# A causal depthwise convolution of width 31: from two chunks on VectorE and six on TensorE to all eight on TensorE, in blocks of 16 channels and 8 shifts

## The chip, the core and the metric

The program runs on one core of a Trainium2 chip. TensorE (PE; its weight loads are shown apart, as PEld) multiplies matrices, VectorE (DVE), ScalarE (ACT) and GpSimd (POOL) work elementwise, and SyncE (SP) issues most of the DMAs. Each engine takes its own instructions in order. The metric is the device time of one execution in microseconds, the median of several runs.

## The reference

One inference step of a two-layer decoder over a new prompt of 512 positions and 8 x 4 sample positions, 544 columns in all, 1024 channels. Layer 0 is a conformer convolution, layer 1 an attention; each is followed by a feed-forward network (FFN). The change lies in layer 0:

```python
def causal_dwconv(x_ext, w, b):           # w: (31, 1024)
    y = lax.conv_general_dilated(x_ext, w[:, None, :], window_strides=(1,), padding='VALID', ...,
                                 feature_group_count=c)
    return y + b

def conformer_conv(h, past, w_in, b_in, w_dw, b_dw, ln_g, ln_b, w_out, b_out):
    u = h @ w_in + b_in
    a, gate = jnp.split(u, 2, axis=-1)
    glu = a * jax.nn.sigmoid(gate)
    ext = jnp.concatenate([past, glu], axis=1)
    y = causal_dwconv(ext, w_dw, b_dw)
    y = jax.nn.silu(layer_norm(y, ln_g, ln_b))
    return y @ w_out + b_out, ext[:, -(CONV_WIDTH - 1):]
```

Each output of a channel is the sum over 31 shifts of that channel's glu times a tap. For the prompt, `past` is zero; the samples have their own past of 30 rows. Layer norm runs over the 1024 channels of a position.

## The kernel before

Activations lie transposed: channels on the 128 partitions, in eight chunks `c`, positions along the free dimension, in two streams `h`: positions 0 to 255 (SA), and 256 to 511 with the 32 samples behind them (SB, 288 columns). Weights come from DRAM as 1 MB blocks `raw`; ACT makes their rounded high part `whi` (line 369), DVE the rest `wlo` (line 372), and a product is three matmuls for each of eight k (lines 700 to 702), into a PSUM tile `acc`. GpSimd's queue issues the loads of `raw` of this layer.

Layer 0 is written as a list of operations given to a planner, `Plan`. Each operation has an engine, a cost, and what it reads and writes; `Plan.run` takes for each engine the ready operation that starts soonest, weighted by rank, and so fixes the order in which every engine's instructions are written (SP's too). On the chip each engine keeps that order and waits at its head.

The steps are: `conv_in` (four products of the input projection, then `glu`, which writes the gated values into `ext_p` behind 30 columns of zeros), the depthwise convolution of the prompt, `conv_sample` (the samples, on DVE: one product of 992 columns and one sum per chunk), `add_sum` (adds the chunks' results `yc`, the same memory as `ext_p`, into `ysum` on DVE), `layer_norm(h)`, and the output projection's products into `xT`. `layer_norm(0)` starts with a matmul by a matrix of 1/1024 (line 870), which gives the mean of every position; then come eight subtractions (line 878), squares, their sums over the channels by four matmuls (line 888), root, reciprocal, eight products (line 899), SiLUs (line 901), and the high and low parts `XH` and `XL` (lines 903 and 904), which the output products take. `layer_norm(1)` does the same for the second half and the samples.

The convolution of the prompt is done in two ways. Chunks 0 and 1 go to DVE (`conv_vector`): 31 operations over 256 or 512 columns, each multiplying a shifted view of `ext_p` with one tap and adding it up (lines 781 to 788). Chunks 2 to 7 go to PE: `shifted` stores a half chunk in DRAM (`glu`) and loads it four times, each time one position further, so that a tile `rep` has four shifts of 32 channels on its 128 partitions, for four groups of channels; `diagonal` makes on ACT, for each group and each of eight steps, a matrix `wdg` of 128 x 32 with the taps on its four diagonals (192 small operations, line 823); `conv_tensor` runs 8 steps x 4 groups of matmuls over 256 columns (line 837; each shows as two records), and ACT evicts the block with the bias into `yc` (line 842). Four `rep` buffers and two PSUM banks `av` go round.

## Time and profile before

| what | us |
|---|---|
| median of three runs (lowest, highest) | 1287.97 (1287.44, 1288.45) |
| the profiled execution | 1289.36 |
| its span on the core | 1287.7 |
| PE busy in the span | 1270.2 (99%) |
| DVE, ACT, POOL busy | 980.4, 713.5, 152.4 |
| matmuls of the convolution (line 837) | 42.9 |
| taps on ACT (line 823) | 42.6 |
| convolution on DVE (line 784, two shapes) | 27.9 + 21.7 |
| first mean over the channels, first half (line 870) | at 135.11 |
| the same, second half and samples | at 165.70 |

The convolution layer takes about the first 219 us; what follows is the first FFN. A line like "L837 PE MATMUL av<-rep,wdg ... x768 | 42.9, 380" is a group: 768 records of line 837, which write `av` from `rep` and `wdg`, busy for 42.9 us together, 380 ns each, overlapping. "[1.30 <-DVE ysum]" in a timeline is idle time of that engine before the instruction, and what ended it.

### The profile page before, as it was taken

The page shows a single profiled execution, that of the slowest core. Times are in us where ns is not written, and L with a number is a line of the kernel's source. Part 1 is how long each engine was busy: PE and PEld are TensorE (multiplying, and loading weights), DVE is VectorE, ACT ScalarE, POOL GpSimd, SP SyncE. Part 2 cuts the span into 40 slices and gives each one's busy share as a digit, 9 for nine tenths or more (in the row PEclk, how much of TensorE's full clock was granted, in tenths as well). Part 3 has the DMA queues.
Part 4 walks back from the last instruction along what each step waited for, and adds up shares of the span by engine and source line. Part 5 has one row for each costly group of instructions (what it writes and reads, how often), then busy time and mean ns, then how long its engine had stood idle before and what let it go on. Part 6 is the DMA issues. An engine that isn't in the chain of part 4 may idle for free.

```text
span 1287.7 us, 26497 instructions
## 1 busy us (share of the span) xinstructions
PE 1270.2 (99%) x10860; PEld 1215.5 (94%) x10860; DVE 980.4 (76%) x1671; ACT 713.5 (55%) x1440; POOL 152.4 (12%) x289
## 2 busy tenths in 40 slices
PE   9999999999999999999999999999999999999997
PEld 8997789999999999999988888889999999999997
DVE  6899875979987877768366586756988987887864
ACT  7596574645644545445366587754645555455453
POOL 4000014101001000000142123100111011000000
PEclk9999999999999999999999999999999999999999
DMA  8465233133232223244553445333133233233221
GB/s 225 123 175 140 83 100 114 34 92 107 91 117 91 91 93 115 67 133 141 175 159 120 140 140 175 104 113 99 50 100 92 93 114 115 67 116 94 80 76 70
DMA packets 119402, 142.38 MB, mean 111 GB/s; under 512 B 5357, under 2 KB 110469, under 8 KB 119010
## 3 DMA queue, kind: packets, MB, share of 16 engines
q1 hardware_dynamic: 110350, 111.89, 28.1%
q0 software_dynamic: 8640, 28.78, 7.1%
q8 instruction: 85, 1.39, 0.5%
q14 instruction: 35, 0.29, 0.1%
q10 hardware_dynamic: 292, 0.02, 0.0%
HBM read 129.34 MB, written 12.18 MB: 110 GB/s over the span
## 4 chain that ended last, share of the span: by engine, by line
PE 85%; DVE 10%; issue 2%; ACT 1%; DMA 1%; DVEq 0%; POOL 0%; ACTq 0%; POOLq 0%
PE acc L1545 5%; PE acc L1543 5%; PE acc L1544 5%; PE acc L700 4%; PE acc L701 4%; PE acc L702 3%; PE acc L459 3%; PE acc L460 3%; PE acc L461 3%; PE tr L1544 3%; PE tr L1543 3%; PE tr L1545 3%; PE av L1341 3%; PE acc L1969 3%; PE av L1343 3%; PE av L1342 3%
## 5 line engine op out<-in xcount | busy, mean ns | idle before, releaser
L372 DVE TENSOR_TENSOR wlo<-raw,whi 128x1024 fp32r<-128x1024 f32 (+2 forms) x245 | 257.4, 1052 | 46.0 <-ACT whi L369 44.5
L369 ACT CAST whi<-raw 128x1024 fp32r<-128x1024 f32 (+2 forms) x245 | 223.5, 914 | 117.1 <-PE av L1342 24.6
L700 PE MATMUL acc<-XH,whi 128*128 128x288 f32 (+1 forms) x384 | 114.5, 298 | 0.0
L701 PE MATMUL acc<-XL,whi 128*128 128x288 f32 (+1 forms) x384 | 110.9, 289 | 0.1
L702 PE MATMUL acc<-XH,wlo 128*128 128x288 f32 (+1 forms) x384 | 110.4, 288 | 0.1
L1969 PE MATMUL acc<-XH,whi 128*128 128x256 f32 (+1 forms) x264 | 82.8, 314 | 0.6 <-ACT XH L2274 0.6
L1543 PE MATMUL acc<-TH,whi 128*128 128x272 f32 x288 | 82.9, 288 | 0.0
L1545 PE MATMUL acc<-TH,wlo 128*128 128x272 f32 x288 | 82.8, 288 | 0.0
L1544 PE MATMUL acc<-TL,whi 128*128 128x272 f32 x288 | 82.7, 287 | 0.0
L1579 ACT COPY G<-acc 128x272 f32<-128x272 f32 (+1 forms) x72 | 26.7, 371 | 94.9 <-PE acc L1545 94.9
L1341 PE MATMUL av<-HH,whi 128*128 128x288 f32 x256 | 76.2, 298 | 0.2
L1970 PE MATMUL acc<-XL,whi 128*128 128x256 f32 (+1 forms) x264 | 76.2, 289 | 0.1
L1971 PE MATMUL acc<-XH,wlo 128*128 128x256 f32 (+1 forms) x264 | 75.9, 287 | 0.0
L1342 PE MATMUL av<-HL,whi 128*128 128x288 f32 x256 | 75.5, 295 | 0.0
L1343 PE MATMUL av<-HH,wlo 128*128 128x288 f32 x256 | 75.3, 294 | 0.0
L700 PEld LDWEIGHTS acc<-XH,whi 128*128 128x128 f32 x384 | 72.2, 188 | 2.8 <-issue 1.6
L701 PEld LDWEIGHTS acc<-XL,whi 128*128 128x128 f32 x384 | 72.3, 188 | 1.0 <-DVE XL L952 0.3
L702 PEld LDWEIGHTS acc<-XH,wlo 128*128 128x128 f32 x384 | 72.2, 188 | 0.3 <-DVE wlo L372 0.3
L1341 PE MATMUL tr<-HH,whi 128*128 128x256 f32 x256 | 71.9, 281 | 0.0
L1342 PE MATMUL tr<-HL,whi 128*128 128x256 f32 x256 | 71.9, 281 | 0.0
L1343 PE MATMUL tr<-HH,wlo 128*128 128x256 f32 x256 | 71.5, 279 | 0.0
L1482 DVE SCALAR_TENSOR_TENSOR cv<-G,fprm,cv 128x560 f32<-128x560 f32 x88 | 69.5, 797 | 0.5
(405 smaller groups left out, 4395.5 us busy)
## 6 DMA issues: line engine op xcount, KB each, us to landing
raw<-in_ffn_w_gate_dram SPq DMA_DIRECT2D x22, 1024.0 KB
raw<-in_ffn_w_up_dram SPq DMA_DIRECT2D x22, 1024.0 KB, 5.4
raw<-in_ffn_w_down_dram SPq DMA_DIRECT2D x24, 768.0 KB, 4.7
raw<-in_attn_w_qkv_dram SPq DMA_DIRECT2D x12, 1024.0 KB, 7.9
raw<-in_conv_w_in_dram POOLq DMA_DIRECT2D x6, 1024.0 KB, 7.8
rep<-glu SPq DMA_DIRECT2D x36, 142.0 KB, 3.7
raw<-in_conv_w_out_dram POOLq DMA_DIRECT2D x4, 1024.0 KB, 6.0
raw<-in_ffn_w_down_dram SPq DMA_DIRECT2D x8, 512.0 KB, 3.4
```

What stands on the lines that cost most here:

```text
L369: act.copy(hi[:, k, :], src[:, k])
L372: dve.tensor_tensor(lo[:, k, :], src[:, k], hi[:, k, :], op=ALU.subtract)
L700: pe.matmul(o, hi[:, k, :], XH[:, k, c0:c0 + n], start=(k == 0), stop=False)
L701: pe.matmul(o, hi[:, k, :], XL[:, k, c0:c0 + n], start=False, stop=False)
L702: pe.matmul(o, lo[:, k, :], XH[:, k, c0:c0 + n], start=False, stop=(k == NC - 1))
L1341: pe.matmul(o, hi[:, j + k, :], xh, start=(start and k == 0), stop=False, **kw)
L1342: pe.matmul(o, hi[:, j + k, :], xl, start=False, stop=False, **kw)
L1343: pe.matmul(o, lo[:, j + k, :], xh, start=False, stop=(stop and k == len(xs) - 1), **kw)
L1543: pe.matmul(o, hi[:, j + k, :], xh, start=(start and k == 0), stop=False, **kw)
L1544: pe.matmul(o, hi[:, j + k, :], xl, start=False, stop=False, **kw)
L1545: pe.matmul(o, lo[:, j + k, :], xh, start=False, stop=(k == 3), **kw)
L1969: pe.matmul(o, hi[:, k, :], XH[:, k, c0:c0 + n], start=(k == 0), stop=False)
```

## The change

All eight chunks go to PE, and the taps are arranged in another way. `glu` now writes `ext_p` with even and odd positions apart (128 even ones, then 128 odd ones, of each half), without zeros in front. For each block of a chunk and a half, `shifted` stores 256 rows of 512 bytes into a DRAM tile `glus` of its chunk, and loads four times 32 partitions: (16 channels x 2 parities) on the partitions, eight groups of 16 channels and up to 140 columns along the free dimension, each load one pair of positions further. A tile `rep` so has 8 shifts of 16 channels. In the first half the columns before position 0 are zeroed by small POOL memsets. `wdg` has for each of 8 groups and 4 steps a matrix of 128 x 32, which gives 16 channels' even and odd outputs at once; DVE makes it in one operation of 1024 columns per block. Where the chunk's matrices have left the four buffers, they are made again; this is so for all second halves, so 16 are made. A block has 2 x 4 x 4 matmuls over 128 columns. Its output partitions are (channel, parity) pairs, so ACT evicts the two PSUM halves with the bias into a tile `ev`, SP stores that in DRAM (`outs`), and loads it back as 128 channels by 256 columns into `yc`. The taps and the biases reach their layout by one load each with rows of 64 bytes and small transposes on PE. Behind the layer norm, the casts and subtractions that make `XH` and `XL` read even and odd columns apart and write them interleaved; the 32 samples have a cast and a subtraction of their own. A list `STEPS` gives the order in which the steps are handed to the planner, and the planner's figure for an SP issue is 0.5 instead of 0.7.

```diff
-PE_CHUNKS = (2, 3, 4, 5, 6, 7)
-WDG_BUFS = 5
+WDG_BUFS = 4
 REPB = 4
+EV_BUFS = 3
+STEPS = (("in", 0, 0), ("in", 0, 1), ("sample", 0, 1), ("shift", 0, 0), ("in", 2, 0), ("conv", 0, 0),
...
+         ("shift", 4, 1), ("conv", 4, 1), ("shift", 6, 1), ("conv", 6, 1))
...
-    for i in range(2):
-        ch0 = (PE_CHUNKS[0] + i * len(PE_CHUNKS) // 2) * P
-        for m in range(8):
-            nj = min(4, CW - 4 * m)
-            pool.dma_start(out=trow[i][m * n_g:(m + 1) * n_g, :nj * 32].rearrange("g (j h) -> g j h", j=nj),
-                          in_=conv_w_dw[0, 4 * m:4 * m + nj, ch0:ch0 + n_g * 32].rearrange("j (g h) -> g j h", h=32))
+    pool.dma_start(out=trow[:, 1:CW + 1, :], in_=conv_w_dw[0].rearrange("k (c i) -> c k i", i=16))
...
+        plan.op("dve", 0.4, lambda: dve.scalar_tensor_tensor(
+            ext_p[:, c, c0:c0 + 256].rearrange("p (f u) -> p f u", f=2),
+            va()[:, :256].rearrange("p (u f) -> p f u", f=2), pcol(R_BIN, c),
+            sg()[:, :256].rearrange("p (u f) -> p f u", f=2),
+            op0=ALU.add, op1=ALU.mult), r=[va, sg, "mix"], w=[("ext", c, h)])
...
-    def conv_vector(c, lo, n):
...
     def shifted(c, h):
+        d = glus[c]
+        r = buf("taps", "rep", [P, 8, WIN], REPB)
+        plan.op("sp", 2.4, lambda: nc.sync.dma_start(
+            out=d[:, :, P * h:P * h + P], in_=ext_p[:, c, 256 * h:256 * h + 256].rearrange("p (f u) -> p f u", f=2)),
+            r=[("ext", c, h)], w=[("glus", c, h)])
         for j in range(4):
+            skip = 0 if h else PAST // 2 - j
+            if skip:
+                plan.op("pool", 0.15, lambda j=j, skip=skip: pool.memset(r()[32 * j:32 * j + 32, :, :skip], 0.0),
+                        r=["taps"], w=[(r, 4 + j)])
+            lo = P * h - PAST // 2 + j + skip
+            plan.op("sp", 4.0, lambda j=j, skip=skip, lo=lo: nc.sync.dma_start(
+                out=r()[32 * j:32 * j + 32, :, skip:],
+                in_=d[:, :, lo:lo + WIN - skip].rearrange("(g i) f v -> (i f) g v", i=16)),
+                r=[("glus", c, k) for k in range(h + 1)] + ["taps"], w=[(r, j)])
...
     def diagonal(c, *r):
-                for i in range(g, g + 4):
-                    act.activation(w()[:, i, :], eye, AF.Copy, scale=t[:, i:i + 1])
+        plan.op("dve", 1.2, lambda: dve.tensor_tensor(
+            w(), eye[:, None, :, None].to_broadcast([P, 32, 16, 2]), t[:, :, None, :].to_broadcast([P, 32, 16, 2]),
+            op=ALU.mult), r=["tapc", "eye", *r], w=[w])
...
     def conv_tensor(c, h, r):
-                        pe.matmul(pt()[32 * g:32 * g + 32, 0:256], wdg()[:, g * 8 + m, :],
-                                  r()[:, g, 4 * m:4 * m + 256], start=(m == 0), stop=(m == 7), skip_group_check=True)
+        if diag.get(c) not in plan.rings.get("wdg", [])[-WDG_BUFS:]:
+            diagonal(c)
...
+                        k = 4 * half + g
+                        pe.matmul(pt()[32 * g:32 * g + 32, P * half:P * half + P],
+                                  wdg()[:, 4 * k + m].rearrange("p i f -> p (i f)"),
+                                  r()[:, k, 4 * m:4 * m + P], start=(m == 0), stop=(m == 3), skip_group_check=True)
...
+        for half in range(2):
+            plan.op("act", 0.23, lambda half=half: act.activation(
+                ev()[:, half, :], pt()[:, P * half:P * half + P], AF.Identity,
+                bias=bcol[:, 2 * c + half:2 * c + half + 1]), r=[pt, "bcol"], w=[(ev, half)])
+        plan.op("sp", 2.2, lambda: nc.sync.dma_start(out=out().rearrange("a p u -> p a u"), in_=ev()),
+                r=[(ev, 0), (ev, 1)], w=[out])
+        plan.op("sp", 2.2, lambda: nc.sync.dma_start(
+            out=yc[:, c, 256 * h:256 * h + 256], in_=out().rearrange("a (i f) u -> (a i) (f u)", f=2)),
+            r=[out, ("glus", c, h), *([("tail", c)] if h else [])], w=[("y", c, h), ("ext", c, h)])
...
+            for z, hi, lo, m in parts:
+                plan.op("act", 0.1 + m * 0.82e-3, lambda z=z, hi=hi: act.copy(hi, z), r=keys, w=[("XH", c, h)])
```

The order of the instructions moves at three places that the prediction speaks of. The numbers behind a name tell buffers apart, and the line numbers are those of each kernel.

PE, the last blocks of the convolution and the start of the output products. Before, four blocks of the second half follow on the input products (`acc_1979`) and the variance matmuls:

```order
L702 MATMUL acc_1979<-XH,wlo_1242 128x288
L837 MATMUL av_2120<-rep_1844,wdg_1061 32x256 x32
L837 MATMUL av_2179<-rep_1913,wdg_1200 32x256 x32
L837 MATMUL av_2234<-rep_1959,wdg_1479 32x256 x32
L837 MATMUL av_2288<-rep_2198,wdg_1669 32x256 x32
L700 MATMUL acc_2335<-XH,whi_1444 128x256
```

Now the last four of the six blocks that come behind the first mean (`av_2092` is chunk 4, `av_2262` chunk 7) stand between the variance matmuls, and the transposes of `tail_p` and `glu_s` ahead of the output products:

```order
L707 MATMUL acc_1802<-XH,wlo_1158 128x288
L821 MATMUL av_2092<-rep_1868,wdg_1809 32x128 x32
L880 MATMUL tr_2022<-sqn_2047,mean_m 128x256
L821 MATMUL av_2137<-rep_1924,wdg_1877 32x128 x32
L880 MATMUL tr_2022<-sqn_2090,mean_m 128x256
L821 MATMUL av_2189<-rep_2016,wdg_2070 32x128 x32
L821 MATMUL av_2262<-rep_2208,wdg_2135 32x128 x32
L1110 MATMUL av_2302<-ident,tail_p 120x128 x2
L1110 MATMUL av_2323<-ident,glu_s 128x128 x2
L705 MATMUL acc_2346<-XH,whi_1396 128x256
```

Only blocks and small matmuls are left there; the input products that stood among them have moved ahead of the first mean.

SP, the end of the convolution's queue. Before, it is stores of glu and loads of `rep`:

```order
L802 DMA glu_2092<-ext_p 128x287
L806 DMA rep_1959<-glu_2092 32x4x284 x2
L802 DMA glu_2151<-ext_p 128x287
L806 DMA rep_1959<-glu_2092 32x4x284
L806 DMA rep_1959<-glu_2092 32x4x283
L806 DMA rep_2198<-glu_2151 32x4x284 x3
L806 DMA rep_2198<-glu_2151 32x4x283
```

Now `outs_2088`, `outs_2180`, `outs_2236`, `outs_2251` and `outs_2313` are the outputs of chunks 3, 4, 5, 6 and 7 of the second half, and `rep_2208` is the input of chunk 7:

```order
L834 DMA ext_p<-outs_2042 128x256
L832 DMA outs_2088<-ev_2074 128x2x128
L784 DMA glus_147<-ext_p 256x1x128
L832 DMA outs_2180<-ev_2157 128x2x128
L832 DMA outs_2236<-ev_2187 128x2x128
L834 DMA ext_p<-outs_2088 128x256
L793 DMA rep_2208<-glus_147 32x8x140 x4
L834 DMA ext_p<-outs_2180 128x256
L832 DMA outs_2251<-ev_2233 128x2x128
L834 DMA ext_p<-outs_2236 128x256
L834 DMA ext_p<-outs_2251 128x256
L832 DMA outs_2313<-ev_2307 128x2x128
```

The loads of `rep_2208` stand behind the stores of chunks 4 and 5.

DVE, from the first half's reciprocal on. Before:

```order
L894 RECIPROCAL dwa_2176<-dwa_2176 128x256
L899 TENSOR_TENSOR ext_p<-ext_p,dwa_2176 128x256 x8
L809 MEMSET rep_2198 32x4
L766 TENSOR_REDUCE ext_p<-prod_2174 128x32
L854 TENSOR_TENSOR ysum<-ext_p,ysum 128x288
L372 TENSOR_TENSOR wlo_2149<-raw_1402,whi_2148 128x1024
L854 TENSOR_TENSOR ysum<-ext_p,ysum 128x288
L904 TENSOR_TENSOR XL<-ext_p,XH 128x256 x3
```

Now:

```order
L886 RECIPROCAL dwa_2206<-dwa_2206 128x256
L891 TENSOR_TENSOR ext_p<-ext_p,dwa_2206 128x256 x8
L766 TENSOR_TENSOR prod_2258<-ext_s,prm 128x992
L846 TENSOR_TENSOR ysum<-ext_p,ysum 128x288
L771 TENSOR_REDUCE ext_p<-prod_2086 128x32
L846 TENSOR_TENSOR ysum<-ext_p,ysum 128x288
L771 TENSOR_REDUCE ext_p<-prod_2258 128x32
L846 TENSOR_TENSOR ysum<-ext_p,ysum 128x288
L378 TENSOR_TENSOR wlo_2178<-raw_1342,whi_2177 128x1024
L846 TENSOR_TENSOR ysum<-ext_p,ysum 128x288
L903 TENSOR_TENSOR XL<-ext_p,XH 128x2x128
L846 TENSOR_TENSOR ysum<-ext_p,ysum 128x288
```

More additions into `ysum` and sample operations stand between the reciprocal and the first `XL`.

183 lines of the change are left out of this document (75 added, 108 removed).

## The prediction

> **What bounds the kernel now.** The page's first part says that PE is busy nearly all the time:
>
> ```profile
> PE 1270.2 (99%) x10860; PEld 1215.5 (94%) x10860; DVE 980.4 (76%) x1671; ACT 713.5 (55%) x1440; POOL 152.4 (12%) x289
> ```
>
> So I read the windows view next, with its cuts at the start of the kernel's steady work, at the wait for the last first-half convolution, and at the two matmuls (line 870) that average the convolution's sums over the channels for the first 256 positions (135.11 us) and for the rest (165.35 us). The columns are stretch, its length, then PE, PEld, DVE, ACT and POOL busy, clock, DMA share, GB/s.
>
> ```profile
> 20.00:115.00 95.00, 95.00 (x863) 88.46 (x866) 84.39 (x164) 72.03 (x249) 7.62 (x9) 1.00 0.53 153
> 115.00:135.11 20.11, 18.81 (x328) 11.63 (x320) 18.91 (x31) 8.26 (x31) 0.00 (x0) 1.00 0.48 115
> 135.11:165.35 30.24, 29.50 (x362) 23.33 (x362) 24.77 (x50) 21.91 (x45) 1.76 (x2) 1.00 0.39 112
> 165.35:219.31 53.96, 52.98 (x410) 51.26 (x411) 38.88 (x66) 31.71 (x64) 17.32 (x21) 1.00 0.34 104
> ```
>
> PE has no hole from 20 to 115 us, and loses 1.3, 0.7 and 1.0 us in the next three stretches. So PE bounds the convolution layer, at full clock, although DVE (84.39 of 95) and ACT are loaded too. After 219.31 us the program is the same in both kernels, and PE is busy there as well, so what the layer gains or loses moves the end one for one. The groups of the first 200 us then say what the convolution itself costs (last columns: busy us, mean ns).
>
> ```profile
> L837 PE MATMUL av<-rep,wdg 128*32 128x256 f32 x768 | 42.9, 380 | 0.6 <-ACT ext_p L901 0.6
> L823 ACT ACTIVATE wdg<-eye,tapc 128x32 f32<-128x32 f32 x192 | 42.6, 308 | 0.0
> L784 DVE SCALAR_TENSOR_TENSOR dwh<-ext_p,prm,dwh 128x256 f32<-128x256 f32 x58 | 27.9, 481 | 1.1
> L784 DVE SCALAR_TENSOR_TENSOR dwa<-ext_p,prm,dwa 128x512 f32<-128x512 f32 x29 | 21.7, 747 | 0.4
> L761 DVE TENSOR_TENSOR prod<-ext_s,prm 128x992 f32<-128x992 f32 x8 | 9.5, 1184 | 0.0
> L842 ACT ACTIVATE ext_p<-av,prm 128x256 f32<-128x256 f32 x12 | 5.5, 462 | 2.5 <-PE av L837 2.4
> ```
>
> Of these only the first lies on the bound: 42.9 us of PE. The 49.6 us of DVE (27.9 + 21.7) and the 42.6 us of ACT lie beside PE and are worth nothing by themselves.
>
> **The PE term.** Before, twelve blocks (six chunks, two halves) have 64 records of 256 columns each. After, sixteen blocks have 64 records of 128 columns. The timeline has the old block, and in a later stage a group with exactly the new shape, 128 rows by 32 columns of weights and 128 moving columns:
>
> ```profile
> 85.43 3.66 PE L837 MATMUL av<-rep,wdg 128*32 128x256 f32 x64
> 89.02 0.40 PE L700 MATMUL acc<-XH,whi 128*128 128x288 f32 x1
> ...
> 89.40 0.29 PE L702 MATMUL acc<-XH,wlo 128*128 128x288 f32 x1
> ...
> 95.40 0.29 PE L702 MATMUL acc<-XH,wlo 128*128 128x288 f32 x1
> ...
> 749.59 1.08 PE L2151 MATMUL dz<-xT 128*32 128x128 f32 x32
> 750.60 0.33 PE L2249 MATMUL t<-ident,e 128*128 128x128 f32 x1
> ```
>
> An old block holds PE 89.02 - 85.43 = 3.59 us. Thirty-two new records hold it 1.01 us with the change-over behind them, so a block of 64 costs at most 2.02; with one change-over of some 0.2 us shared, 1.8 at least. I take 1.9: 16 x 1.9 = 30.4 against 12 x 3.59 = 43.1, so 12.7 us less PE work. From 89.40 to 95.40 there are 45 products of 288 columns, 0.133 each.
>
> The 1.01 us for 32 records are 32 ns each, so a record of 128 columns is not held at the old record's 3.59 / 64 = 56 ns. [...]
>
> **Where that gain can be kept.** In the new order PE reaches the first mean (I call this T0) with ten blocks done instead of eight, and with 12 products of the input projection left instead of 84. T0 = 135.11 - 1.3 (the wait before it, below) + 72 x 0.133 - 8 x 3.59 + 10 x 1.9 + 0.6 = 134.3. The 0.6 is for twelve small matmuls that turn taps and bias in place of two, at 0.05 to 0.1 each by these rows of the chain:
>
> ```profile
> 53.18 0.17 PE av L1018 x2
> 53.35 0.41 PE av L1054 x4
> ```
>
>  Its inputs are there: behind the last first-half block stand 54 products (7.2 us) before T0, and its eviction, store, load and one addition take 5 to 6, at the prices below. DVE and ACT have 50 and 40 us less to do by then; the sixteen diagonals now on DVE cost about 1.18 each by line 761 (a broadcast of much the same size), 14 of them (17 us) before T0, in place of 49.6. So T0 moves by under 1 us: PE spends what the blocks save on the products that it used to do later.
>
> Between the two means PE then has left 12 x 0.133 + 6 x 1.9 + four variance matmuls and small transposes (about 3.5) = 16.5 us, where it had 28. But two chains pass through that stretch and must end before the second mean, and these rows price them:
>
> ```profile
> 135.11 0.70 PE L870 MATMUL tr<-ysum,mean_m 128*128 128x256 f32 x2 [1.30 <-DVE ysum L854]
> 165.70 0.75 PE L870 MATMUL tr<-ysum,mean_m 128*128 128x288 f32 x2 [0.45 <-DVE ysum L854]
> ...
> 135.85 1.42 DVE L878 TENSOR_TENSOR ext_p<-ext_p,tr 128x256 f32<-128x256 f32 x4 [0.79 <-PE tr L870]
> 146.53 1.18 DVE L761 TENSOR_TENSOR prod<-ext_s,prm 128x992 f32<-128x992 f32 x1
> 153.14 1.74 DVE L894 RECIPROCAL dwa<-dwa 128x256 f32<-128x256 f32 x1
> 154.91 2.78 DVE L899 TENSOR_TENSOR ext_p<-ext_p,dwa 128x256 f32<-128x256 f32 x8
> 160.82 1.09 DVE L904 TENSOR_TENSOR XL<-ext_p,XH 128x256 fp32r<-128x256 f32 x3
> ...
> 148.82 1.98 ACT L369 CAST whi<-raw 128x1024 fp32r<-128x1024 f32 x2
> 150.93 1.28 ACT L446 ACT_TABLE_LOAD   x1
> 155.65 1.09 ACT L901 ACTIVATE ext_p<-ext_p,prm 128x256 f32<-128x256 f32 x2
> 156.65 0.70 ACT L903 CAST XH<-ext_p 128x256 fp32r<-128x256 f32 x2
> ```
>
> The page's DMA issues (median us to landing), and the view of the tile `rep` (duration of an issue and landing, each min/median/max):
>
> ```profile
> rep<-glu SPq DMA_DIRECT2D x36, 142.0 KB, 3.7
> ...
> glu<-ext_p SPq DMA_DIRECT2D x6, 143.0 KB, 1.8
> ```
>
> ```profile
> L806 SPq DMA_DIRECT2D rep<-glu x48: 302/430/1666, 56.2 to 156.8; - x48
> ...
> DMA to landing us min/median/max: 2.5/3.7/7.0
> ```
>
> The chain of the last block (chunk 7, second half), counted from T0. Its gates and values come from 12 products, two blocks and two variance matmuls: T0+6.5. DVE has eight subtractions (2.8), three additions (1.0), two gate products (0.8), one diagonal and one sample product (2.3) ahead of the GLU: T0+8, so its glu is in DRAM at T0+10. That doesn't decide. SP takes its queue in order, and ahead of this block's four loads stands the store of block (5, second half). PE ends that block at T0+10.6; its two evictions stand on ACT behind two weight casts (1.9), a table load (1.28) and a variance root: T0+12.2. Four issues of 0.43 (the median of 302/430/1666), the fourth at T0+14.3, and 3.7 to landing: the block runs from T0+18 to T0+19.9. Before, the eviction went straight to SBUF and the mean followed in about 2 us. Now: two evictions (0.6, each below the 0.46 of line 842 for half the columns), a store (I take 1.8, as glu<-ext_p, of like size), an issue of 0.4, a load of 1.8 to 2.2, one addition of 0.4: the second mean can start at T0+25.5.
>
> The layer-norm chain of the first half runs alongside: root at about T0+11.5, reciprocal to 13.7, the products to 16.5; the first two SiLUs and casts, behind a table load, the eviction of block (6, second half) and a cast of weights (1.28 + 0.6 + 1.0), end at about T0+17, but the DVE order puts two sample products and sums, a weight difference and five additions ahead of the low halves: 23 to 24 us after T0. So PE does its twelve output products just before the second mean, and sits idle for about 25.5 - 16.5 = 9 us of this stretch. That is where the 12.7 us go.
>
> From T0+25.5 I add 0.9 for transfers above their medians (a load has twice the rows of half the length now): T0+26.4 = 160.7, in place of 165.35, -4.6 us. Behind it 53.96 us remain for output products and the second layer norm. The change adds 8 casts and 8 subtractions of 32 columns and strided writes there, some 3.5 us of ACT and DVE; PE is the bound in that stretch (52.98 of 53.96), and of this I let 0.7 show: -4.6 + 0.7 = -3.9 us.
>
> The unknown costs and their bounds. Strided reads and writes of 256 columns: at the price of the plain rows (0.35 cast, 0.34 subtraction) or twice that; only 16 casts and 16 differences near the two norms matter: 0 to 3 us. The loads of 560-byte rows where there were 1136: 2.5 to 7.0, taken 3.7, as the bytes are the same. The load of the taps, now in rows of 64 bytes, is wanted only by the transposes near 53 us (line 1018, above), where PE has been busy without a hole: nothing, at worst 1. The profiled execution took 1289.36 us around a span of 1287.7; -3.9 gives 1285.5 there. The three timed runs have their median 1.4 lower, 1287.97, so I predict 1284 for it.
>
> **The rivals.** (1) *The waits overlap better, and PE stays the bound.* Speaks for it: every chain has only single transfers at 1.8. If the DVE and ACT orders cost me 4 us less than counted, the second mean comes at T0+22 instead of T0+26.4: -3.9 - 4.4 = -8.3 us, 1279.7. (2) *The DRAM way decides, and the kernel is slower.* Place: SP's single queue, with seven DMAs per block instead of five and sixteen blocks instead of twelve, 112 for 60. Each wait for an eviction holds all behind it. With the last loads at 7.0 instead of 3.7 (+3.3), the two last legs 1.6 later each (+3.2) and T0 itself late by 2.6, the change costs -3.9 + 9.1 = +5.2, 1293. It decides from about 4 us of lateness on. For: the 7.0 was seen with fewer DMAs. Against: in the last stretch few transfers are in flight. (3) *The two cancel*: 2 to 5 us of lateness, 1286 to 1289, no difference that can be told. (4) *A floor for each record*, as if it cost the old 56 ns whatever its width: 16 x 3.59 = 57.4, +14.3 us on PE for -12.7. Ten of the blocks lie before T0 (+16.9 us against my sum there); of the other six's +10 us the 9 us of idleness take most: -3.9 + 16.9 + 1 = +14, 1302. Line 2151 speaks against it. [...]
>
> **How the numbers follow.** Forecast 0.42, around 1284 with its own range 1281 to 1286; rival 1 0.14; rival 2 0.18; rival 3 0.23; rival 4 0.03. The range 1278 to 1293 leaves out the far ends of rivals 1 and 2 and rival 4, about 0.15. A measurement of this kernel can tell about 0.2% (2.6 us): faster means under 1285.4, slower over 1290.5. Faster: 0.42 x 0.87 + 0.14 + a little of rival 3 = 0.53. Slower: rivals 2 and 4 with a little of rival 3: 0.22. The rest, 0.25, is the same.
>
> **What would show it.** Right: blocks of 64 records in 1.8 to 2.0 us; the first mean at 133 to 136 us and the second about 26 after it; PE with 6 to 10 us of idle time between them, ended by a load of `rep` or by the ysum addition; SP waiting there for ACT. Wrong: an idle PE before the first mean (rival 2 begins early), a second mean within 23 us of the first (rival 1), or blocks near 3.6 us (rival 4). The prediction falls if PE idles more than 13 us in the layer, or if the stretch behind the second mean grows by over 3 us.

## The result and the profile after

The changed kernel takes 1308.1 us (median; 1306.4 to 1308.8) beside 1288.2 us before: a ratio of 1.0152 with a 95% interval of 1.0135 to 1.0170. It is slower by 19.9 us, where 4 us less were forecast; the range (1278 to 1293) doesn't hold it. The profiled spans are 1304.7 and 1287.7 us, 17.0 apart.

The windows view of the changed kernel, cut at the same events as before (start of steady work, the first mean, the second mean, and the end of the layer; columns as in the prediction):

```profile
20.00:115.00 95.00, 93.58 (x988) 90.36 (x988) 54.41 (x83) 38.40 (x80) 11.30 (x35) 1.00 0.65 159
115.00:148.47 33.47, 24.38 (x420) 22.50 (x418) 17.47 (x27) 7.47 (x22) 0.73 (x4) 0.95 0.72 177
148.47:182.18 33.71, 21.60 (x423) 17.84 (x423) 24.58 (x47) 23.09 (x52) 1.77 (x2) 0.86 0.58 161
182.18:236.07 53.89, 53.75 (x406) 52.50 (x406) 41.77 (x78) 31.67 (x69) 17.36 (x20) 0.96 0.33 100
```

The layer ends at 236.07 in place of 219.31 us: 16.8 of the span's 17.0. The first mean (T0) comes at 148.47 where 134.3 was forecast, the second 33.71 behind it where 26.4 was; what follows takes 53.89 for 54.7. PE idles 1.4 + 9.1 + 12.1 + 0.1 = 22.7 us in these stretches, and its clock, 1.00 throughout before, is below 1 in three of them.

**Where the lateness begins.** The wait list of DVE (what it stood at, and for whom; total us, times, longest) and DVE's timeline at the longest of these waits:

```profile
DVE ysum L846 <- DMA ext_p<-outs: 32.0, 6, 13.3
```

```profile
97.06 1.22 DVE L805 TENSOR_TENSOR wdg<-eye,tapc 128x1024 f32<-128x1024 f32 x1
111.60 0.42 DVE L846 TENSOR_TENSOR ysum<-ext_p 128x256 f32<-128x256 f32 x1 [13.32 <-DMA ext_p<-outs]
111.94 1.18 DVE L766 TENSOR_TENSOR prod<-ext_s,prm 128x992 f32<-128x992 f32 x1
113.05 0.45 DVE L734 TENSOR_TENSOR sg<-acc,rstd 128x288 f32<-128x288 f32 x1
```

DVE stands 13.3 us at the first addition of returned outputs, and a gate product (line 734) of another chunk stands behind it: it starts at 113.05 us, while PE's last matmul of 288 columns ahead of it had ended at 99.65, and PE then waits 1.4 us for it; with that the GLU, the store, the loads and the blocks of the later chunks come late. The chain of waits up to the first mean says what the addition waited for (start, length, what):

```profile
97.90 7.43 DMA rep<-glus
105.35 6.23 DMA ext_p<-outs
...
122.09 3.27 DMA glus<-ext_p
127.40 2.59 DMA glus<-ext_p
...
137.01 4.84 DMA outs<-ev
144.82 3.15 DMA ext_p<-outs
148.47 0.70 PE tr L862 x2
```

Loads of `rep` take 7.4 us where I priced 3.7, the load back 6.2 and 3.2 for 1.8 to 2.2, a store of outputs 4.8 and one of glu 3.3 for 1.8. SP's timeline says why this load back starts only at 105.35 us:

```profile
86.42 10.92 SPq L832 DMA_DIRECT2D outs<-ev  x3
97.50 2.16 SPq L793 DMA_DIRECT2D rep<-glus  x4
99.76 0.90 SPq L834 DMA_DIRECT2D ext_p<-outs  x1
100.75 4.49 SPq L793 DMA_DIRECT2D rep<-glus  x4
105.35 0.39 SPq L834 DMA_DIRECT2D ext_p<-outs  x1
```

SP stands at three stores, from 86 to 97 us, until their evictions are done, and then eight loads of `rep` and an earlier load back go ahead of this one. So of the 13.3 us for which DVE stands (from 98.3 us), some 7 are SP's queue and 6.2 the transfer.

Why are the transfers slow? The DMA view from 86 to 112 us, first of the kernel before, then of the changed one (q1 carries what SP issues, q0 the weight loads of GpSimd's queue):

```profile
DMA packets 1772, 3.40 MB, mean 131 GB/s; under 512 B 160, under 2 KB 1256, under 8 KB 1768
q1 hardware_dynamic: 1224, 1.25, 19.0%
```

```profile
DMA  0079599950600000006778899999999999999999
GB/s 0 0 206 109 183 410 334 397 189 0 202 0 0 0 25 0 0 0 191 87 170 267 312 401 326 300 147 175 213 191 163 166 152 229 192 172 176 150 186 218
DMA packets 4724, 4.31 MB, mean 166 GB/s; under 512 B 1821, under 2 KB 4208, under 8 KB 4720
q1 hardware_dynamic: 4176, 2.17, 49.6%
```

From about 101 us on the DMA engines are full (a digit is a fortieth of the stretch, 0.65 us), and behind 103 us, when a weight load has ended, they move only 147 to 229 GB/s. The packets of the hardware queues went from 1224 to 4176 in the same 26 us, their bytes from 1.25 to 2.17 MB. Per packet, on 16 engines, that is 0.190 x 16 x 26 us / 1224 = 65 ns before, for some 1021 B, and 0.496 x 16 x 26 us / 4176 = 49 ns now, for some 520 B. The 49 ns are not what a packet of this size has to cost: the packets of the store in the last leg, below, have some 480 B and take 0.080 x 16 x 5.5 us / 272 = 26 ns, and from 112 to 135 us q1, with nothing on q0, moves 6378 packets and 3.35 MB (some 525 B each) with 58.2% of the engines, 0.582 x 16 x 23 us / 6378 = 34 ns each. So loads of "the same bytes" are not loads of the same time here; what makes the packets dear in this stretch is not shown.

**The last leg.** The chain of waits ahead of the second mean:

```profile
166.22 3.79 DMA rep<-glus
170.14 3.33 PE av L821 x64
173.49 0.63 ACT ev L829 x2
174.15 5.45 DMA outs<-ev
179.61 1.93 DMA ext_p<-outs
181.66 0.47 DVE ysum L846
182.18 0.85 PE tr L862
```

Loads and load back are as priced; the store takes 5.45 us for 1.8, and the block 3.33 for 1.9. The DMA view from 174.0 to 179.5 us shows the store's company, a weight load of 1 MB:

```profile
DMA packets 544, 1.18 MB, mean 215 GB/s; under 512 B 32, under 2 KB 288, under 8 KB 544
q0 software_dynamic: 272, 1.05, 50.7%
q1 hardware_dynamic: 272, 0.13, 8.0%
```

The store's 0.13 MB need 8.0% of the engines, but they lie among packets of about 4 KB (1.05 MB in 272). The small store lasts about as long as the large load (5.45 us, and 5.8 from the load's issue to its landing), and e8, below, which moves an eighth of these loads, has 1.81 us for it. The trace has 272 / 16 = 17 records per engine for either transfer, but in which order an engine takes them is not shown.

**The clock.** The windows view at PE's waits and behind them (clock is the third column from the end):

```profile
118.50:121.70 3.20, 0.05 (x4) 0.00 (x0) 2.56 (x4) 0.98 (x3) 0.73 (x4) 1.00 0.57 146
121.73:125.14 3.41, 3.02 (x60) 2.80 (x64) 2.77 (x6) 1.36 (x5) 0.00 (x0) 0.50 0.29 81
149.03:152.44 3.41, 3.41 (x65) 2.96 (x64) 3.41 (x10) 1.08 (x3) 0.88 (x1) 0.50 0.59 123
164.20:169.40 5.20, 0.10 (x4) 0.00 (x0) 5.17 (x12) 5.19 (x13) 0.00 (x0) 1.00 0.85 198
169.52:172.93 3.41, 2.79 (x55) 2.82 (x59) 3.41 (x5) 1.50 (x4) 0.00 (x0) 0.50 0.27 80
176.30:179.70 3.40, 0.13 (x2) 0.00 (x0) 0.00 (x0) 2.73 (x6) 0.00 (x0) 1.00 0.74 287
179.76:186.58 6.82, 4.40 (x18) 4.12 (x19) 4.63 (x11) 2.55 (x5) 0.00 (x0) 0.50 0.18 49
```

Behind the waits of 3.56, 2.48, 5.84 and 5.75 us PE's clock is 0.50 for 3.41 us or twice that, so PE is slow exactly when the awaited data is there. The four stretches are 17 us at half clock in the layer. The stretches start 27.30, 20.49 and 10.24 us apart, which is 8, 6 and 3 times 3.413 us, the length of the shorter ones. In the 3.41 us ahead of the stretch at 149.03 us PE was still busy for 0.93 us. By what rule the clock falls is not shown.

### The profile page after: what moved, and what is told of

Its sections match the earlier page's. It is cut to its first block, busy times and chain, and to the rows that moved or that the text cites. A ratio compares the mean times of both kernels' runs of the same rounds, so it can differ in the third digit from the quotient of the medians.

```text
span 1304.7 us, 26907 instructions
## 1 busy us (share of the span) xinstructions
PE 1265.9 (97%) x11130; PEld 1222.3 (94%) x11130; DVE 951.7 (73%) x1594; ACT 680.3 (52%) x1276; POOL 154.0 (12%) x305
## 4 chain that ended last, share of the span: by engine, by line
PE 81%; DVE 11%; DMA 4%; issue 1%; ACT 1%; SPq 1%; DVEq 0%; POOL 0%; ACTq 0%; POOLq 0%
PE acc L1540 5%; PE acc L1538 5%; PE acc L1539 5%; PE acc L705 3%; PE acc L466 3%; PE acc L465 3%; PE acc L467 3%; PE acc L706 3%; PE acc L707 3%; PE tr L1538 3%; PE tr L1540 3%; PE tr L1539 3%; PE av L1336 3%; PE acc L1964 3%; PE av L1338 3%; PE av L1337 3%
```

## The experiments

Times are medians; in brackets the difference to the kernel before, timed beside it, and the ratio's 95% interval. The changed kernel itself stands at +19.9. Where nothing else is said, the order of instructions on PE and DVE is row for row that of the changed kernel.

### Is it the way back at all?

e1 leaves the way back out, and the planner, which doesn't see it any more, makes a new order:

```diff
-            ev()[:, half, :], pt()[:, P * half:P * half + P], AF.Identity,
+            yc[:, c, 256 * h + P * half:256 * h + P * half + P], pt()[:, P * half:P * half + P], AF.Identity,
...
-        plan.op("sp", 2.2, lambda: nc.sync.dma_start(out=out().rearrange("a p u -> p a u"), in_=ev()),
-                r=[(ev, 0), (ev, 1)], w=[out])
-        plan.op("sp", 2.2, lambda: nc.sync.dma_start(
-            out=yc[:, c, 256 * h:256 * h + 256], in_=out().rearrange("a (i f) u -> (a i) (f u)", f=2)),
```

> Leaves out the way back through DRAM: the evictions write their 128 columns straight into the convolution's output tile, so the outputs stand in permuted channels and times; all other work is the same. Theory A, the return way (two evictions, a store, a load, one queue in order) makes PE wait: PE's seven gaps of over 1 us between 111 and 182 us nearly vanish, first mean at 135 to 139 us (148.5 in the changed kernel), second 24 to 28 us behind it, 1284 to 1291 us in all. Theory B, the way out (glus stores and the four rep loads of 500-byte rows) makes PE wait: first mean stays at 143 to 148 us and the total at 1300 to 1308 us. Theory C, the clock: whatever gaps remain, each is followed by a stretch of half clock; without gaps none is seen in the layer.

1284.7 us (-4.5; 0.9954 to 0.9974). The way back, with the order made for it, costs 24 us, and without it the blocks' gain is there. Its first mean comes at 128.2 us, earlier than expected, and PE has no gap of over 1 us ahead of it; the second is 30.7 behind, not 24 to 28. Part of both is the order: e1 leaves 66 products (single matmuls, as the prediction counts them) between the means, the changed kernel 24, and 42 x 0.133 = 5.6 us; counted with the changed kernel's order, the first mean would come at 133.8 us and the second 25.1 behind it. So theory A, and C in part: two gaps of 3 us remain between the means (one of 3.33, up to 157.76 us), each followed by half clock.

e14 keeps the order and the planner's entries, and issues nothing in them (the evictions write into `yc`, as in e1); e15 does so for the first half's blocks alone:

```diff
-        plan.op("sp", 2.2, lambda: nc.sync.dma_start(out=out().rearrange("a p u -> p a u"), in_=ev()),
+        plan.op("sp", 2.2, lambda: None,            # e15: None if h == 0, else as before
...
-        plan.op("sp", 2.2, lambda: nc.sync.dma_start(
+        plan.op("sp", 2.2, lambda: None,            # the load back, likewise
```

> The changed kernel's order of work on every engine, kept, with the 32 transfers of the way back alone left out (evictions go straight to the output tile, so channels and times are permuted). If the 23 us are the waiting for returned outputs: 1284 to 1290 us, DVE's waits at the additions under 5 us. If the order that the planner makes with the transfers in it costs by itself: 1293 to 1302 us, with gaps of PE left before its blocks.

> As the run with the order kept, but only the first half's eight blocks leave out the way back; the second half's outputs still go through DRAM. If both halves' waits are paid at PE: first mean 8 to 14 us earlier than 148.5, the two gaps of 6 us ahead of the last block and the second mean stay, 1294 to 1300 us. If the second half's chain alone sets the end: first mean earlier, the second mean at 178 to 182 as before, 1303 to 1308 us.

e14: 1290.8 us (+1.9; 1.0003 to 1.0023). e15: 1296.5 us (+7.5; 1.0038 to 1.0068). The transfers by themselves cost 18.0 us, 12.4 of them in the first half and 5.6 in the second; the order that was made with them in it costs 6.4 more (e14 against e1). e14 lies just over the first range forecast for it, and DVE waits at the additions for 1.6 us in all. The first mean comes at 140.78 us in e14 and at 141.07 in e15, 7.7 and 7.4 us earlier than with the transfers. In e14's windows DVE has 63.61 us done by 115 us, in place of 54.41:

```profile
20.00:115.00 95.00, 95.00 (x1002) 91.85 (x1000) 63.61 (x96) 40.45 (x88) 11.29 (x35) 1.00 0.62 157
115.00:140.78 25.78, 23.42 (x413) 22.13 (x412) 10.59 (x16) 5.55 (x15) 0.73 (x4) 0.93 0.75 143
```

### Queues, legs, or the DMA engines?

e2 issues the stores from ACT's queue; e5 also issues the loads back from POOL's:

```diff
-        plan.op("sp", 2.2, lambda: nc.sync.dma_start(out=out().rearrange("a p u -> p a u"), in_=ev()),
+        plan.op("sp", 2.2, lambda: act.dma_start(out=out().rearrange("a p u -> p a u"), in_=ev()),
...
-        plan.op("sp", 2.2, lambda: nc.sync.dma_start(
+        plan.op("sp", 2.2, lambda: pool.dma_start(            # the load back, e5 only
```

> Only the 16 stores of evicted outputs are issued from ACT's queue, directly behind their evictions, in place of SP's; the order on PE and DVE is the same. Theory A1, SP's order: stores and loads behind a waiting store hold each other up, so the gap of 3.8 us at 118 us (PE waits for an eviction, whose buffer waits for a store) goes, and the two last gaps of 6 us shrink by 1 to 3 us each: 1298 to 1303 us. Theory A2, the transfers themselves: their own 2 to 5 us decide, the total stays at 1306 to 1310 us, with ACT's 16 issues of about 0.5 us (8 us) hidden beside PE.

> The whole return way leaves SP's queue, with the order on PE and DVE as it was: the 16 stores are issued from ACT's queue, the 16 loads back from POOL's. Theory A1, a wait in SP's queue holds up what is behind it: DVE's 13.3 us at the first addition (98.3 to 111.6 us) fall to 5 or less, the first mean comes at 138 to 144 us in place of 148.5, 1294 to 1301 us. Theory A2, the transfers' own time: 1305 to 1311 us, as with the stores alone on ACT.

e2: 1309.4 us (+20.1; 1.0131 to 1.0165). e5: 1310.1 us (+21.9; 1.0147 to 1.0181). No gain in either: SP's order alone is not the cause. In e2's chain of waits the load back, now issued 7 us earlier, takes 10 us to land; the first mean comes at 151.7 us, no earlier than in the changed kernel:

```profile
98.09 10.07 DMA ext_p<-outs
```

In e5 DVE's longest wait at an addition falls from 13.3 to 5.4 us, but the waiting has moved to POOL, whose queue also holds the memsets of `rep` and the weight loads:

```profile
POOL ext_p L834 <- DMA outs<-ev: 62.4, 9, 15.2
```

e3 and e11 go from SBUF to SBUF in one leg of four transfers, from SP's queue and (with the additions on POOL) from ACT's; both have an order of their own:

```diff
+        for f in range(2):
+            for a in range(2):
+                nc.sync.dma_start(        # e11: act.dma_start
+                    out=yc[64 * a:64 * a + 64, c, 256 * h + P * f:256 * h + P * f + P], in_=ev()[f::2, a, :])
```

> The outputs go back from SBUF to SBUF in four transfers of 64 partitions per block, with no store to DRAM and no wait of a load for it; SP issues 144 transfers in place of 112. Theory A2, the two legs through DRAM decide: the way from the last block's eviction to the second mean falls by about 4 us (9.0 us from the block's last matmul to the mean in the changed kernel), the first mean comes 4 to 8 us earlier, 1296 to 1302 us. Theory A1, SP's queue decides: 32 more issues of 0.4 to 0.7 us are 13 to 22 us more on the queue in the layer, the gaps stay or grow, 1307 to 1318 us.

> Additions on POOL, and the way back in one leg: four transfers per block from SBUF to SBUF, issued from ACT's queue directly behind the evictions; SP issues only the way out (80 transfers in place of 112). Theory A1/A2 together (a leg too many, and a queue that waits): last block's end to the second mean 4 to 6 us in place of 9.0, first mean at 132 to 138 us, 1288 to 1294 us. If ACT's 64 issues of 0.37 to 0.5 us (24 to 32 us, in a stretch where ACT is 23 of 34 us busy) or the 64-row transfers cost as much: 1297 to 1303 us.

e3: 1315.3 us (+26.1; 1.0161 to 1.0215). e11: 1323.3 us (+34.6; 1.0237 to 1.0278). The rival expectation in both, and in e11 beyond it. The first row is from e3's view of the tile `ev`, the second from ACT's timeline in e11:

```profile
L833 SPq DMA_DIRECT2D ext_p<-ev x64: 464/540/1606, 66.7 to 184.5; - x64
```

```profile
101.82 5.01 ACTq L834 DMA_DIRECT2D ext_p<-ev  x4
```

64 issues of 0.54 us are 35 us on SP; on ACT four of them took 2.4 to 5.0 us, and a cast, a copy and an eviction behind them waited for 2.73, 4.82 and 3.20 us.

e8 takes the company away: the four weight loads of 1 MB move an eighth.

```diff
-            pool.dma_start(out=t[:, :nk, :], in_=src)
+            pool.memset(t[:, 1:, :], 0.0)
+            pool.dma_start(out=t[:, :1, :], in_=src[:, :1, :])      # the four loads of conv_w_out
```

> Leaves out seven eighths of each of the four 1 MB loads of output-product weights (a POOL memset fills the rest, so the products are of wrong numbers; all other work is the same). Theory E, the small packets of the return way wait behind the 4 KB packets of these loads: the last leg (store issued at 174.15, load at 179.61 us) falls from 5.5 to 2 to 3 us, as may others near 90, 100 and 155 us: 2 to 5 us less, 1303 to 1306 us. Theories A1 and D alone: 1306 to 1309 us.

1302.6 us (+14.3; 1.0090 to 1.0124), 5.6 us less, a little past the far end of theory E. Its chain ahead of the second mean has the store at the price that I had taken:

```profile
171.30 1.81 DMA outs<-ev
```

e9 makes all rows of the first half's loads 560 bytes long and drops POOL's memsets (the order shifts in places):

```diff
-    glus = [scratch.tile([P, 2, 256], F32, name=f"glus{c}") for c in range(NC)]
+    glus = [scratch.tile([P, 2, ZP + 256], F32, name=f"glus{c}") for c in range(NC)]      # ZP = 16 zeros, stored once
...
-            skip = 0 if h else PAST // 2 - j
+            skip = 0
```

> Sixteen zeros are stored once ahead of each chunk's rows in DRAM, so that the first half's rep loads are whole rows of 560 bytes like the second half's; the 32 memsets of rep on POOL are gone. Theory F, rows of 500 to 508 bytes are slow and POOL's memsets hold up loads: the first half's blocks come earlier and the time falls by 3 to 8 us, 1300 to 1305 us. Rival, the way back decides whatever the way out costs: 1305 to 1310 us.

1301.8 us (+13.1; 1.0076 to 1.0110), 6.8 us less: theory F's figure. Since memsets, row lengths and in part the order changed together, how the gain divides stays open.

### DVE's queue and the planner's costs

e7 moves the additions to POOL, e6 tells the planner longer transfers, e10 does both. Each has an order of its own.

```diff
-            dve.tensor_tensor(o, yc[:, c, c0:c0 + n], yc[:, 0, c0:c0 + n] if c == 1 else o, op=ALU.add)
+            pool.tensor_tensor(o, yc[:, c, c0:c0 + n], yc[:, 0, c0:c0 + n] if c == 1 else o, op=ALU.add)      # e7, e10
...
-    plan.issue = 0.5
+    plan.issue = 0.7      # e6, e10; glus 2.4 to 3.0, rep 4.0 to 5.0, outs 2.2 to 4.0 both ways
```

> The fourteen additions that sum the chunks' outputs run on POOL in place of DVE, so that nothing of the gated unit or the diagonals is queued behind one that waits for a returned output; POOL's memsets and weight loads now are. Theory D: DVE's 32.0 us at the additions go, PE's idle time before the first mean (12 us) falls to 5 or less and the first mean comes at 138 to 143 us: 1296 to 1302 us; the two last gaps of 6 us stay. Theory A2: 1305 to 1310 us. If POOL's memsets of the repeated rows stand behind a waiting addition, the rep loads come later: 1308 to 1315 us.

> Only the planner's costs of the five kinds of transfer are changed (an issue 0.7 in place of 0.5, glus store 3.0, rep load 5.0, store and load of the outputs 4.0 each), and by them the order on all engines. Theory D, DVE's additions stand too early in its queue (32.0 us in which DVE waits at them for returned outputs, the gate products, diagonals and GLU of other chunks queued behind): with later additions the wait at them falls under 15 us and PE's idle time in the layer (22.7 us) under 14: 1296 to 1302 us. Theory A2: the transfers' own time is the same whatever the order, 1304 to 1310 us.

> The additions on POOL and the planner's higher transfer costs together, the way through DRAM kept. Theory D with A1 (the way back hurts by standing in the engines' queues ahead of other work): the two gains, 8 us and 5 us alone, add at least in part, 1293 to 1298 us. If both took away the same wait (DVE's 13 us at the first addition): 1298 to 1302 us, as POOL's additions alone.

e7: 1299.8 us (+11.5; 1.0068 to 1.0102). e6: 1303.0 us (+14.7; 1.0087 to 1.0136). e10: 1305.7 us (+17.1; 1.0115 to 1.0160). Freeing DVE from the waiting additions is worth 8.4 us, with the first mean at 143.9: theory D, as far as it goes. PE still idles 6.5 us ahead of that mean in e7, where 5 or less were expected. The order by longer costs is worth 5.2: DVE's waits for returned outputs fall to 10.7 us, as theory D has it, but PE idles 17.2 us between 20 and 240 us, not under 14, and the time lies between the two ranges. Together the two edits give 2.8, less than either: an expectation missed on both sides. What an edit of the order is worth here hangs on the order that comes out, and the single gains must not be added.

### The clock by itself

e4 puts 158 matmuls of zeros (bf16, 256 columns) ahead of six instructions that wait; e16 has 28 behind the block before in place of e4's 26 ahead of the block at 122 us. The edit shown is e16's:

```diff
+    KEEP = {("end", 5, 0): 28, (6, 0): 6, (7, 0): 16, ("mean", 0): 18, (7, 1): 44, ("mean", 1): 48}
+    def keep_warm(o, key):
+        for i in range(KEEP.get(key, 0)):
+            pe.matmul(o[:, :w], zero[:, :P], zero[:, :w], start=True, stop=True)      # o: unused columns of the bank
```

> The same work with 158 small matmuls of zeros added on PE ahead of six instructions that wait (bf16, 256 columns, about 0.11 us each, 17 us in all, placed into the waits of 3.8, 1.1, 2.5, 2.8, 6.1 and 6.0 us); their results are not read. Theory C, the clock that falls to half after each wait is a cost of its own: the 17 us at half clock in the layer vanish, and the time falls by up to 8 us, to 1300 to 1304 us. Rival, the half clock lies where PE would wait anyway: 1306 to 1311 us, with the clock at 1.00 in the layer.

> As the run with added matmuls of zeros, but the 28 ahead of the block at 122 us now stand behind the block before it, where they wait for no PSUM bank and so should delay nothing. Clock as a cost of its own: 1.00 throughout the layer and 1298 to 1301 us, 7 to 10 us under the changed kernel. If the matmuls delay as much as the clock gains: 1301 to 1304 us, as the run before.

e4: 1301.0 us (+11.8; 1.0071 to 1.0105). e16: 1300.8 us (+11.8; 1.0082 to 1.0113). Eight us less, from more work on PE. e16's windows, cut at its own means and end of the layer:

```profile
115.00:147.25 32.25, 30.21 (x483) 27.11 (x481) 17.07 (x26) 7.09 (x21) 0.73 (x4) 1.00 0.73 186
147.25:177.75 30.50, 28.45 (x515) 24.03 (x514) 24.23 (x47) 23.05 (x52) 1.76 (x2) 1.00 0.66 177
177.75:229.80 52.05, 51.96 (x406) 50.76 (x406) 41.57 (x78) 31.55 (x69) 17.33 (x20) 1.00 0.33 103
```

The clock stays at 1.00. The first mean comes 1.2 us earlier, the second follows it 3.2 sooner, and what follows takes 1.8 less: 6.2 us in the layer, and 7.4 in the profiled spans (1297.3 for 1304.7). PE was busy for 3.02 + 3.41 + 2.79 + 4.40 = 13.6 of the 17 us at half clock, so these can cost some 6.8 us at most (an estimate from the clock of 0.50; a block in them took 3.56 us for 1.95), and nearly all of it was paid in the layer. Theory C, as a cost of its own; the waits themselves are still there.

### Outputs put in place without a transfer

The blocks' rows can be ordered so that a return never leaves a group of 32 rows. In e13 block k = 2g + a holds channels 32g + 16a to 32g + 16a + 15, its PSUM rows are (parity, channel) for a = 0 and the parities exchanged for a = 1. Even outputs then lie in their own rows; odd ones are exchanged by sixteens with one DVE shuffle.

```diff
-                        k = 4 * half + g
+                        k = 2 * g + half
...
+        for f in range(2):                               # lanes: 0/1 masks of the lower and upper 16 rows
+            act.activation(ev()[:, f, :], pt()[:, P:2 * P], AF.Identity, scale=lanes[:, 1 - f:2 - f],
+                           bias=bcol[:, c:c + 1] if f else pcol(R_BDW, c))
+        for f in (1, 0):
+            dve.scalar_tensor_tensor(ev()[:, f, :] if f else y[f], pt()[:, 0:P], lanes[:, f:f + 1], ev()[:, f, :],
+                                     op0=ALU.mult, op1=ALU.add)
+        dve.stream_shuffle(out=y[1], in_=ev()[:, 1, :], mask=[(i + 16) % 32 for i in range(32)])
```

> The full result without a way back: a block gives for each group of 32 PSUM rows 16 channels in the upper or lower 16 rows by parity; ACT evicts one half twice under a row mask, DVE adds the other half under the opposite mask, and one DVE shuffle within groups of 32 rows exchanges the two sixteens of the odd outputs. DVE gets three operations of 128 columns per block (48, some 0.25 us each, 12 us), SP 32 transfers fewer. If the way back is the cause and its work in other form is hidden beside PE: 1281 to 1287 us, as without it (1284.7). If 12 us more of DVE work show on the way to the means: 1288 to 1295 us.

1287.3 us (-1.6; 0.9976 to 0.9994): faster than both kernels, against the one before at the edge of what can be told, and between the two ranges forecast for it. The groups view prices the masked addition (the other one is alike, 344) and the shuffle (mean ns of one, after the comma):

```profile
L832 DVE SCALAR_TENSOR_TENSOR ev<-av,lanes,ev 128x128 f32<-128x128 f32 x16 | 5.5, 345 | 0.9 <-ACT ev L826 0.8
L835 DVE STREAM_SHUFFLE ext_p<-ev 128x128 f32<-128x128 f32 x16 | 4.7, 296 | 0.0
```

With 15.7 us more for DVE (12 expected) it is busy for 28.6 of the 32.1 us between the means. e17 has the additions on POOL besides, e18 a lower lift of the first mean in the planner (5 for 10), and e19 adds 58 matmuls of zeros to e17:

> The shuffling kernel with the fourteen additions of the sums on POOL: 6 us less for DVE, about half of it between the means. If DVE's queue holds PE there: second mean 28 to 30 us behind the first in place of 32.1, 1281 to 1285 us. If another engine or the loads hold it: 1286 to 1289 us.

> As the last, with the planner's lift of the first mean at 5 in place of 10, so that more of the second half's work may stand before the first mean. If the stretch between the means holds too much DVE and ACT work for PE's share: the first mean later by 1 to 4 us, the second earlier by 1 to 3, 1280 to 1284 us. If the order does not matter there: within 1 us of the last.

> The shuffling kernel with additions on POOL, and 58 added matmuls of zeros on PE: 46 behind the block that ends at 146.5 us (4.9 us, in a wait of 5.8 us) and 12 ahead of the second mean (1.2 us, in a wait of 1.8). If the half clock behind the wait is paid: 3.4 us less at most, 1281 to 1283.5 us. If the second mean waits for DVE, ACT and POOL anyway: 1284 to 1286 us, with the clock at 1.00 in the layer.

e17: 1284.9 us (-4.2; 0.9951 to 0.9978), the fastest of those that put the outputs in their places, and 24 us under the change as it was made. But not by the reason given: its second mean is 33.4 us behind the first, not 28 to 30, and why it is faster than e13 is open. In e18, with more work ahead of the first mean, the means come at 142.8 and 167.8 us and the time is 1291.9 (+2.8; 1.0016 to 1.0037): wrong in sign. e19: 1288.3 us (-1.0; 0.9984 to 1.0002), slower than e17 although its added matmuls should have hidden in a wait. ACT's waits in e19 name the reason (line 802 is the added matmul):

```profile
ACT ev L837 <- PE av L802: 4.9, 1, 4.9
```

The 46 matmuls write unused columns of the block's own PSUM tile, and the eviction behind them waited for the tile. Its clock is still 0.50 for 6.83 us, from 157.74 us on. So e19 doesn't tell what the half clock costs in e17; that stays open.

## Why the prediction was wrong

**Right.** The block at full clock: 64 records in 1.9 us, between 1.8 and 2.0 (3.3 to 3.6 where the clock was at half).

```profile
110.17 1.96 PE L821 MATMUL av<-rep,wdg 128*32 128x128 f32 x64
```

That is some 30 ns per record, so rival 4's 56 ns for each don't hold here. The sum of PE's own work was right as well: in e1, where PE has no gap of over 1 us ahead of the first mean, this mean comes at 133.8 us when counted with the changed kernel's order, 134.3 in the sum, and the whole is 4.5 us faster, 3.9 in the sum. (That e17 gains 4.2 is no second proof: its means come at 130.6 and 164.0 us.) The stretch behind the second mean agrees in part by luck, 53.89 us for 54.7: 4.4 us of PE's work in it ran at half clock, and e16, at full clock, has 52.05. Between the means the chain that I laid out (last loads, block, evictions, store, load back, addition) is the one that the trace shows.

**The step that failed** is "*Its inputs are there*", T0 = 134.3; the first mean came at 148.47. The sum has the last first-half block start 7.2 + 1.9 us ahead of T0, at 125.2 us; it started at 136.6. The step went wrong in two ways. First, I priced only the last block's eviction, store, load and addition ("take 5 to 6"; from that block's end at 138.6 us it took 9.9) and didn't ask what stands behind the addition of each earlier chunk on DVE. The first of them held DVE for 13.3 us, and with it the gates, the glu and the loads of the later blocks. Second, I took the transfers at the medians of a kernel whose hardware queues kept the DMA engines 19% busy between 86 and 112 us, and the `rep` loads at 3.7 us "as the bytes are the same". With 1.7 times the bytes in 3.4 times as many packets these queues took 50%, the engines were full from 101 us on, and transfers took 1.4 to 3 times their price. Of the 14.2 us at T0, 7.7 go when the way back issues no transfer (e14, at 140.78 us); of the 6.5 that stay, a wait of 2.4 us for loads of `rep` and the half clock behind it show in e14's trace, and the rest is not traced. In the whole time the first half's transfers cost 12.4 us (e15).

**Between the means** 33.7 us for 26.4. The start of the last block (T0+18 foreseen, T0+21.7 measured) is 3.7 of this, its half clock 1.4, the store beside a weight load 3.6, less 1.4 elsewhere. The store I had priced by a row from a time without such company (1.8; e8 measures 1.81 without it). The clock I hadn't considered at all, though I had forecast 9 us of idleness in this stretch: a wait of PE that the sum books as free time is here, from 2.48 us on, followed by 3.4 us or more at half speed. e16 prices that at 6 us in the layer and 8 in the whole time. Of the 3.7 us, 2.7 were there when PE ended the block of chunk 5, whose store stands ahead of the last loads (161.8 us, T0+13.3 for T0+10.6 foreseen): the first block behind the mean had run at half clock, 3.56 us for 1.9. On SP a load back of 1.05 us stood ahead of those loads besides.

**The rivals.** Rival 2 had the sign and the kind of cause, with 0.18, but not its size (1293) nor its place. It put the wait into SP's queue, and there some 7 of DVE's 13.3 us do lie; but e2 and e5 took the way back off SP and gained nothing, as the transfers then took longer or the wait moved. Its T0 was late by 2.6 us, not 14.2. The order itself, 6.4 us by e14 against e1, was in none of my cases: the planner was told 2.2 us for each leg and put the additions where the outputs would have been.

Two of the signs that I named for being wrong came: PE idle ahead of the first mean, and 22.7 us of idleness in the layer, over 13.

**What stays open:** how the 18.0 us of the transfers divide between DVE's queue (8.4 by e7), the company of the weight loads (5.6 by e8), the clock (8 by e16), and the short rows and memsets (6.8 by e9). These overlap, since a wait that goes takes its half clock with it (in e16, where matmuls fill the waits, the clock is 1.00 in the layer), and e10 shows that they don't add. It is also open why packets of some 480 to 525 B took 49 ns in one stretch and 26 and 34 in two others.

## What to carry to other kernels

Price a moved transfer by how full the DMA engines will be in that stretch, not by the median of a quieter kernel (here, with the engines full from 101 us on, transfers took 1.4 to 3 times it), and ask of every consumer that waits for it what stands behind on that engine's queue. Count a longer wait of PE twice: once as idle time, once as the stretch of half clock behind it (in the changed kernel's layer the four waits of 2.48 us and more were each followed by one of 3.41 or 6.82 us, those of 2.22 us and less were not). Where a result has only to change rows within a group of 32, choose the layout of the blocks so that a DVE shuffle of 0.3 us does it, and no round trip through DRAM.

## What the runs showed of the hardware

- A wait of PE of only 2.48 us was followed by half clock, although the first mean was already running behind it, and in e14 so was one of 2.36 us; one of 2.22 us in the changed kernel, up to 136.63 us, was not. PE's timeline in the changed kernel, at the stretch from 149.03 us:

```profile
148.47 0.70 PE L862 MATMUL tr<-ysum,mean_m 128*128 128x256 f32 x2 [2.48 <-DVE ysum L846]
149.10 3.56 PE L821 MATMUL av<-rep,wdg 128*32 128x128 f32 x64
```

- Some 160 matmuls of zeros, in waits of PE, made a kernel faster by 8 us (e4, e16); 58 of them made another slower by 3.2 us (e19 against e17), where an eviction waited 4.9 us for the tile that they wrote to.
- A store of 128 KB took 1.81 us alone (e8, where the view from 164 to 173 us has no packet on q0) and 5.45 us beside a load of 1 MB in packets of some 4 KB (the changed kernel).
- A DVE shuffle of 128x128 f32 within groups of 32 rows took 296 ns, less than the 345 ns of a masked addition that reads PSUM (e13).
